# Hybrid decoder trunk: later slots for q's rstd transposes, attention steps one QKV item later, a fourth HGRN unit on unnormalised x

## The chip, the cores and the metric

The kernel runs as one program on one core of a Trainium2 chip. The metric is the device time of one execution in microseconds (us); three runs of the kernel before have a median of 2326.11 us. TensorE is called PE, VectorE DVE, ScalarE ACT, GpSimd POOL, and SyncE SP. SP issues nearly all loads.

## The reference, cut to what matters

Two layers work on a sequence of 256 tokens of width 2048 in f32. Every layer is a mixer and then a squared-ReLU MLP, each behind an RMS norm with shift, scale and gate that come from a conditioning vector. Layer 0 mixes by attention in a window of 128 tokens, layer 1 by a gated linear recurrence (HGRN2).

```python
for i in range(DEPTH):
    mod = cond @ mod_w[i] + mod_b[i]
    sh1, sc1, g1, sh2, sc2, g2 = jnp.split(mod, N_MOD, axis=-1)
    h = modulate(rms_norm(x, norm_mix[i]), sh1, sc1)
    ...
        y = swa_sink_attention(h, ...)     # layer 0
        y = hgrn2_mixer(h, ...)            # layer 1
    x = x + g1[:, None, :] * y
    h = modulate(rms_norm(x, norm_mlp[i]), sh2, sc2)
    x = x + g2[:, None, :] * squared_relu_mlp(h, mlp_w1[i], mlp_w2[i])
```

In attention, q and k get an RMS norm per head of 64 columns before the logits. In HGRN2 one projection gives q, f, v and g for 16 heads. From f come the decay and k, g gates the output, and the recurrence runs in chunks of 64 tokens.

## The kernel before

**Weights.** Every weight and every row of `mod_w` is loaded once, in pieces of 1 MB, in the order of a list that is written out by hand (`seq`, filled by `put`, L144). The pieces go through a ring of `NRAW` = 5 buffers called `raw`, and SP issues the next load when a buffer comes free. An item of kind "w" is a weight: ACT rounds each half of it to `wh`, DVE subtracts that from the original and gets `wl` (L252), and PE multiplies with both; `wh` and `wl` have 5 buffers of half an item each. An item of kind "m" is a column group of `mod_w`: one DVE instruction multiplies it with the conditioning vector and sums (L234). An item of kind "g" is another form of the same, done by PE in four small matmuls, which the profile counts as eight, with four transposes behind every fourth item (`gemv`, L259). `put` takes a function `per(i)`, which says how many such modulation items stand in the list before weight `i`.

**Order.** The program is written as one stream in Python, and a scheduler turns it into one fixed order for each engine; an instruction that is not ready by its model may be passed by later ones. Matmuls issued through `pep` are tied to the PE instruction before them, those through `pe` are not. Work that has to wait for another engine is put off with `later(n, fn)`: it is issued n slots on, and a slot passes with each call of `hook`. A unit of 32 matmuls (`mm_std`) has four slots, and so has a quarter unit of QKV (`mm_quarter`). An attention step has two.

**QKV and attention.** The projection runs in four sections, one for each quarter of the width (`s_` = 0 to 3, L863). Each has five items `e`: item 0 is k and v, items 1 to 4 are q, two tiles of four heads to an item. Only section 3 completes the sums. For the q norm, `evac_q` (L701) squares both tiles of an item; then `f1` (one slot on) sums by PE, `f2` (one slot on) turns the sums by PE transposes (`sst`), computes rstd on DVE in 13 small instructions and widens it by two copies (`widen`, L663). `f3`, once for each tile, turns the wide rstd back by four PE transposes (`spread`, tile `rbk`) and multiplies q with it (L726).

Attention is a pipeline of steps (`step`, L820). Step s forms the logits of head pair s (tile `S`), from step 1 on scales the pair before on POOL, from step 3 on transposes pair s-3 (`pt`), from step 4 on multiplies pair s-4 with v (`pv`), and from step 9 on runs the output projection for its first four tiles (`wo_step`, 12 matmuls each). Step s needs the normed q of tile s // 2. Each step also prepares up to two modulation items. With `EE` = 1 and `SE` = 3, three steps run after each of the items 2, 3 and 4 of section 3, and steps 9 to 20 run in a loop behind them. While `hold` is set, the preparation of weights does not go past a modulation item on its own.

**HGRN.** Each of 8 groups of two heads has 8 units: f, f, g, v, v, q, g, q. `start_phase` (L1032) begins the phase while the norm is still being computed: its first `count` units (`UN` = 3: f, f, g) run on x times gain and scale without rstd (`u`, three matmuls for each of 16 steps instead of two), and are multiplied with rstd afterwards. Meanwhile DVE and ACT make the 16 normed tiles `h`, with three instructions each. The first v unit is the first that needs them. Behind each q unit, `evac_hq` (L1128) computes the scaled q and k of a head into `qa`, `ka`, `qb` and `kd`, with one buffer each, and `stage1` (five slots on) has PE read them. `put` for the items `hin` (L195) spreads 32 modulation items of kind "m" over the units from item 4 on.

Of the kernel before, what the change touches and what calls it, by code (L numbers as in the profile page):

```python
# [27 lines left out]
LAG = 2  # L28
DT = 3
DV = 1  # L30
UN = 3
# [2 lines left out]
NCST = 553  # L34
LEAD = 2
GPS = 2
EE = 1
SE = 3
GD = 2


# [22 lines left out]
def trunk(ctx, tc, a, out):  # L64
# [107 lines left out]
    for c in range(3):  # L172
# [1 line left out]
        put([a["ainq"][c, i] for i in range(5)], nxt, per=lambda i: 2 * i)  # L174
    both = [e for p in zip(gga, two(0, SC2, SH2, 0, KH)) for e in p]
    put([a["ainq"][3, i] for i in range(5)] + [a["aoutk"][i] for i in range(4)], both,
        per=lambda i: (0, 0, 0, 6, 12, 18, 22, 26, 32)[i])
    order = [("o", n) for n in range(4, 12)]
    late = [("o", n) for n in range(12, 16)]
    half1 = [("u", n) for n in range(8)]  # L180
# [8 lines left out]
    for c in range(NCHUNK):  # L189
# [3 lines left out]
    put(rest, mods_of(0, G2) + two(1, SC1, SH1, 0, KB) + mods_of(1, G1),  # L193
        per=lambda i: max(0, i - 16) * 64 // 84)
    put([a["hin"][i] for i in range(64)], two(1, SC2, SH2, 0, KB),  # L195
        per=lambda i: max(0, i - 4) * 32 // 56)
    put([a["hout"][n] for n in range(16)])
    rest = []
    for c in range(NCHUNK):
# [120 lines left out]
    def later(delay, fn):  # L320
        bg.append((bgst["slot"] + delay, bgst["n"], fn))
        bgst["n"] += 1
        bg.sort(key=lambda e: (e[0], e[1]))
# [283 lines left out]
    H = feed.H  # L607
# [4 lines left out]
    with tc.tile_pool(name="attn", bufs=2) as ap:  # L612
# [88 lines left out]
        def evac_q(i, ps, part):  # L701
            dve.tensor_tensor(out=part, in0=ps, in1=part, op=ALU.add)
            sq = wt(2 * T)
            act.activation(out=sq, in_=part, func=AF.Square)
            for u in range(2):
                qts[2 * i + u] = part[:, u * T:(u + 1) * T]
                sqs.append(sq[:, u * T:(u + 1) * T])
            if i % 2 == 0:
                return
            four = sqs[:]  # L710
            sqs.clear()

            def f1():
                fin = head_rstd(four, slope2[:, 4 * i - 4:4 * i + 4])
                later(1, lambda: f2(fin))

            def f2(fin):
                r = fin()
                rxs = [widen(r, k) for k in range(2)]
                later(2, lambda: f3(rxs, 0))  # L720
                later(3, lambda: f3(rxs, 1))

            def f3(rxs, k):
                rb = spread(rxs[k])
                q = parts[i + 1 + k]
                dve.tensor_tensor(out=q, in0=q, in1=rb, op=ALU.mult)  # L726
                rq[i - 1 + k] = True
            later(1, f1)
# [364 lines left out]
    def f_tile(h):  # L1093
        if h % 2 == 0:
            cur["fl"] = htile("fl", 2, 2 * T)
            cur["kk"] = htile("kk", 2, 2 * T)
        c = slice((h % 2) * T, (h % 2 + 1) * T)
        fk[h] = (cur["fl"][:, c], cur["kk"][:, c])
        return fk[h][0]

    def g_tile(h):
        gts[h] = htile("g", 3)
        return gts[h]
# [16 lines left out]
    def evac_g(h):  # L1120
        g = gts[h]
        th = wt()
        act.activation(out=th, in_=g, func=AF.Tanh, scale=0.5)
        dve.scalar_tensor_tensor(out=g, in0=th, scalar=1.0, in1=g, op0=ALU.add, op1=ALU.mult)
        dve.tensor_scalar(out=g, in0=g, scalar1=0.5, scalar2=ogain[:, h:h + 1],
                          op0=ALU.mult, op1=ALU.mult)
# [89 lines left out]
    def evac_fg(r, h, ps):  # L1216
        if r < 2:
            total(ps, f_tile(h))
            evac_f(h)
        else:  # L1220
            total(ps, g_tile(h))
            evac_g(h)

    H, n0 = start_phase(1, 0, UN, lambda i: f_tile(i) if i < 2 else g_tile(i - 2),
                        lambda i, t: evac_f(i) if i < 2 else evac_g(i - 2))
    for i in range(n0, 64):
        G, r = divmod(i, 8)
        if r < 2:
            mm_std(H, lambda ps: evac_fg(0, 2 * G + r, ps))
        elif r in (2, 6):  # L1230
            mm_std(H, lambda ps: evac_fg(2, 2 * G + (r - 2) // 4, ps))
        elif r == 3:
            ps = mmtile()
            mm_v(H, 0, ps, True, False)
            ahead(LAG - 1, False)
        elif r == 4:
            mm_v(H, 1, ps, False, True)
            vn = hp.tile([P, 2, T], F32, tag="vn", name="vn", bufs=2)
            act.copy(out=vn.rearrange("p a b -> p (a b)"), in_=ps)
            vns[G] = vn  # L1240
            ahead(LAG - 1, False)
        else:
            mm_std(H, lambda ps: evac_hq(2 * G + (r - 5) // 2, ps))
    mod_bias(1, G1)
    prep_mods(1, SH2)
    prep_mods(1, SC2)
# [12 lines left out]
def layout(inputs):  # L1259
    import numpy as np  # L1260

    def units(w, nk):
        k, n = w.shape
        u = w.reshape(nk, KB, P, n // P, P).transpose(3, 0, 2, 1, 4)
        return np.ascontiguousarray(u.reshape((n // P) * nk, P, D))

    f = np.float32
    i = {k: np.asarray(v) for k, v in inputs.items()}
    r = {}
    r["x"] = np.ascontiguousarray(i["x"][0].T.reshape(4, 4, P, T).transpose(0, 2, 1, 3))  # L1270
    def gset(col):
        g = i["mod_w"][0][:, col * P:(col + 4) * P].reshape(4, 4, P, 2 * T)
        return g.transpose(0, 2, 1, 3).reshape(4, P, D)

    r["mod_g"] = np.stack([gset(c) for c in (0, 4, 8, 12, 32, 36, 40, 44)])
    r["mod_w"] = np.ascontiguousarray(i["mod_w"].transpose(0, 2, 1).reshape(2, 96, P, D))
    gs = np.stack([i["norm_mix"][0], i["norm_mlp"][0], i["norm_mix"][1], i["norm_mlp"][1]])
    def halves(u):
        n = u.shape[0]
        v = u.reshape(n // 2, 2, P, 2, D // 2).transpose(3, 0, 2, 1, 4)  # L1280
        return np.ascontiguousarray(v.reshape(2, n // 2, P, D))

    def vpairs(w):
        v = w.reshape(2, KB // 2, P, w.shape[1] // T, T).transpose(3, 0, 2, 1, 4)
        return np.ascontiguousarray(v.reshape(-1, 2, P, D))

    win = i["attn_w_in"][0]
    ku, qu, wv = units(win[:, D:D + T], 1), units(win[:, :D], 1), win[:, D + T:]
    def quarter(k0):
        c = slice(k0 * P, (k0 + 4) * P)  # L1290
        kv = [*ku[:, :, c], wv[k0 * P:(k0 + 4) * P].reshape(4, P, T).transpose(1, 0, 2).reshape(P, 4 * T)]
        q = qu[:, :, c].reshape(4, 4, P, 4 * P).transpose(0, 2, 1, 3).reshape(4, P, D)
        return np.concatenate([np.concatenate(kv, 1)[None], q], 0)
    r["ainq"] = np.stack([quarter(k0) for k0 in range(0, KB, 4)])
    wo = i["attn_w_out"][0]
    r["aoutk"] = np.ascontiguousarray(
        wo[:, :4 * P].reshape(4, 4, P, 4 * P).transpose(0, 2, 1, 3).reshape(4, P, D))
    r["aout"] = units(wo[:, 4 * P:], 1)
    hu = units(i["hgrn_w_in"][0], 1)
    hv = vpairs(i["hgrn_w_in"][0][:, 2 * D:3 * D])  # L1300
    hs = []
    for h in range(0, HG, 2):
        hs += [hu[16 + h], hu[17 + h], hu[48 + h], hv[h // 2, 0], hv[h // 2, 1], hu[h],
               hu[49 + h], hu[h + 1]]
    r["hin"] = np.stack(hs)
    r["hout"] = units(i["hgrn_w_out"][0], 1)
    m1 = units(i["mlp_w1"][0], 1)
    r["m1h"] = halves(m1[:16])
    r["mlp1a"] = np.ascontiguousarray(m1[16:])
    r["mlp1b"] = units(i["mlp_w1"][1], 1)  # L1310
    r["mlp2"] = np.stack([units(i["mlp_w2"][l], NCHUNK) for l in range(2)])
    kg, qg = i["attn_k_gain"][0], i["attn_q_gain"][0]
    sel = np.zeros((P, 2), f)
    sel[:HD, 0] = 1
    sel[HD:, 1] = 1
    slope = 2.0 ** (-8.0 * np.arange(1, HEADS + 1) / HEADS)
    rows = np.concatenate([i["attn_sinks"][0], (-slope).astype(f), (slope * slope / HD).astype(f),
                           np.full(4, 1.0 / HD, f)])
    cst = [i["c"].reshape(KB, P).T, np.eye(P, dtype=f), sel,
           (np.arange(P) % 32 == 0).astype(f).reshape(P, 1),  # L1320
           np.stack([np.concatenate([kg, kg]), np.concatenate([qg, qg])], 1),
           i["hgrn_o_gain"][0].T,
           np.broadcast_to(rows, (P, rows.size)),
           i["hgrn_lb_logits"].reshape(2, HG, P).transpose(2, 0, 1).reshape(P, 2 * HG),
           gs.reshape(4, KB, P).transpose(2, 0, 1).reshape(P, 4 * KB),
           i["mod_b"].reshape(2, 96, P).transpose(2, 0, 1).reshape(P, 192)]
    r["cst"] = np.concatenate(cst, 1)
    q = np.arange(P)[:, None]
    s = np.arange(P)[None, :]
    ok = s <= q  # L1330
    cur = np.where(ok, -(q - s), -1e38)
    prev = np.where(s > q, -(q + P - s), -1e38)
    r["dist"] = np.concatenate([prev, cur], 1).astype(f)
    cm = np.arange(P)[:, None] <= np.arange(P)[None, :]
    r["cmask"] = np.concatenate([cm, cm], 1).astype(np.int32)
    return r
# [20 lines left out]
```

## Time and profile before

| | us |
|---|---|
| median of 3 runs | 2326.11 (2325.68 to 2327.92) |
| the profiled execution, its own time | 2325.76 |
| span from its first to its last instruction | 2324.0 |
| PE busy | 2265.4 |
| DVE busy | 1792.2 |
| ACT busy | 1161.4 |

The profile has a page with sums and several views: busy time of each engine in stretches of time, waits by who ended them, groups of instructions by line, a timeline, and the chain of work that ended last. The busy time of PE is modelled from overlapping matmuls. PEclk is the clock that was granted to PE as a share of the full one. Idle time of an engine matters only where nothing else sets the end.

### The profile page before, as it was taken

The page shows a single profiled execution, that of the slowest core. Times are in us where ns is not written, and L with a number is a line of the kernel's source. Part 1 is how long each engine was busy: PE and PEld are TensorE (multiplying, and loading weights), DVE is VectorE, ACT ScalarE, POOL GpSimd, SP SyncE. Part 2 cuts the span into 40 slices and gives each one's busy share as a digit, 9 for nine tenths or more (in the row PEclk, how much of TensorE's full clock was granted, in tenths as well). Part 3 has the DMA queues.
Part 4 walks back from the last instruction along what each step waited for, and adds up shares of the span by engine and source line. Part 5 has one row for each costly group of instructions (what it writes and reads, how often), then busy time and mean ns, then how long its engine had stood idle before and what let it go on. Part 6 is the DMA issues. An engine that isn't in the chain of part 4 may idle for free.

```text
span 2324.0 us, 37074 instructions
## 1 busy us (share of the span) xinstructions
PE 2265.4 (97%) x14690; PEld 1988.7 (86%) x14690; DVE 1792.2 (77%) x2908; ACT 1161.4 (50%) x1962; POOL 107.8 (5%) x94
## 2 busy tenths in 40 slices
PE   5998899999999999999999999999999999999999
PEld 3885699988888888888889988999888888888888
DVE  5787798957888988988988988767766766655665
ACT  3544554644444444455666666655544444444443
POOL 0244510000000000000000000000000000000000
PEclk8998999999999999999999999999999999999999
DMA  9987799557898998975677777554666666555552
GB/s 357 399 324 276 284 351 337 203 186 269 324 335 322 331 329 329 329 288 184 219 274 268 255 269 269 186 174 171 235 237 228 242 235 233 202 185 196 181 199 91
DMA packets 84638, 598.80 MB, mean 258 GB/s; under 512 B 9456, under 2 KB 11504, under 8 KB 12272
## 3 DMA queue, kind: packets, MB, share of 16 engines
q1 hardware_dynamic: 81936, 593.81, 70.6%
q8 instruction: 115, 1.88, 0.3%
q10 hardware_dynamic: 2304, 2.10, 0.3%
q0 software_dynamic: 224, 0.52, 0.1%
q14 instruction: 59, 0.48, 0.1%
HBM read 594.04 MB, written 2.10 MB: 257 GB/s over the span
## 4 chain that ended last, share of the span: by engine, by line
PE 93%; DVE 4%; DMA 2%; ACT 1%; issue 1%; POOL 0%; DVEq 0%; ACTq 0%
PE mm L52 88%; DVE wl L252 1%; DVE raw L234 1%; PE A L52 1%; DMA raw<-in_mod_w_dram 1%; PE S L52 1%; PE on L52 0%; PE pt L52 0%; ACT wh L52 0%; PE pv L52 0%; DMA raw<-in_aoutk_dram 0%; DMA raw<-in_ainq_dram 0%; ACT h L52 0%; PE rbk L52 0%; PE cb L52 0%
## 5 line engine op out<-in xcount | busy, mean ns | idle before, releaser
L252 DVE TENSOR_TENSOR wl<-raw,wh 128x1024 fp32r<-128x1024 f32 x744 | 914.3, 1234 | 398.9 <-ACT wh L52 397.3
L52 ACT CAST wh<-raw 128x1024 fp32r<-128x1024 f32 x744 | 778.1, 1051 | 877.5 <-PE mm L52 768.0
L52 PE MATMUL mm<-h,wh 128*128 128x512 f32 (+2 forms) x3728 | 1150.7, 367 | 15.6 <-ACT wh L52 14.5
L52 PE MATMUL mm<-h,wl 128*128 128x256 f32 (+1 forms) x3232 | 906.4, 281 | 1.0 <-DVE wl L252 1.0
L52 PE MATMUL mm<-o,wh 128*128 128x512 f32 (+2 forms) x3120 | 859.0, 346 | 1.2 <-ACT o L52 0.9
L52 PEld LDWEIGHTS mm<-h,wh 128*128 128x128 f32 x3728 | 668.7, 189 | 143.2 <-ACT wh L52 15.3
L52 PE MATMUL mm<-o,wl 128*128 128x256 f32 (+1 forms) x2432 | 678.5, 280 | 0.0
L52 PEld LDWEIGHTS mm<-h,wl 128*128 128x128 f32 x3232 | 610.4, 189 | 8.2 <-issue 5.4
L52 PEld LDWEIGHTS mm<-o,wh 128*128 128x128 f32 x3120 | 538.7, 188 | 82.9 <-issue 2.2
L52 PEld LDWEIGHTS mm<-o,wl 128*128 128x128 f32 x2432 | 457.2, 188 | 0.7 <-issue 0.3
L234 DVE CUSTOM_DVE_ANT_0 raw<-raw,cond 128x2048 f32<-128x2048 f32 x160 | 368.9, 2306 | 25.5 <-DMA raw<-in_mod_w_dram 25.2
L52 ACT COPY w<-mm 128x256 f32<-128x256 f32 (+1 forms) x308 | 118.2, 386 | 24.0 <-PE mm L52 24.0
L52 PE MATMUL mm<-wh,h 128*128 128x256 f32 x576 | 106.8, 285 | 4.2 <-DVE h L553 2.7
L52 PEld LDWEIGHTS mm<-wh,h 128*128 128x128 f32 x576 | 89.8, 190 | 7.8 <-DVE h L553 3.2
L52 PE MATMUL mm<-wl,h 128*128 128x256 f32 x288 | 81.4, 283 | 0.0
L772 POOL TENSOR_SCALAR h<-h,asm 128x128 f32<-128x128 f32 x64 | 66.0, 1049 | 65.1 <-DVE qw L137 28.2
L52 ACT CAST h<-w 128x256 fp32r<-128x256 f32 x125 | 49.8, 403 | 27.5 <-DVE w L969 26.7
L52 PEld LDWEIGHTS mm<-wl,h 128*128 128x128 f32 x288 | 54.7, 190 | 0.2
L969 DVE SCALAR_TENSOR_TENSOR w<-w 128x256 f32<-128x256 f32 x125 | 52.2, 423 | 2.2
L478 DVE TENSOR_TENSOR h<-w,h 128x256 fp32r<-128x256 f32 x125 | 51.7, 419 | 0.0
L474 DVE TENSOR_TENSOR w<-mm,w 128x256 f32<-128x256 f32 x109 | 45.6, 419 | 0.4 <-ACT w L52 0.3
L990 DVE TENSOR_TENSOR acc<-mm,acc 128x256 f32<-128x256 f32 x96 | 40.6, 423 | 6.4 <-PE mm L52 3.5
(191 smaller groups left out, 1091.1 us busy)
## 6 DMA issues: line engine op xcount, KB each, us to landing
raw<-in_mod_w_dram SPq DMA_DIRECT2D x160, 1024.0 KB, 6.3
raw<-in_mlp_dram SPq DMA_DIRECT2D x128, 1024.0 KB, 4.9
raw<-in_hin_dram SPq DMA_DIRECT2D x64, 1024.0 KB, 5.0
raw<-in_mlp1b_dram SPq DMA_DIRECT2D x64, 1024.0 KB, 4.8
raw<-in_mlp1a_dram SPq DMA_DIRECT2D x48, 1024.0 KB, 6.4
raw<-in_mod_g_dram SPq DMA_DIRECT2D x32, 1024.0 KB, 6.9
raw<-in_ainq_dram SPq DMA_DIRECT2D x20, 1024.0 KB, 7.6
raw<-in_m1h_dram SPq DMA_DIRECT2D x16, 1024.0 KB, 6.7
```

The costliest lines, as they stand in the source:

```text
L52: r = fn(*args, **kw)
L234: dve.tensor_tensor_reduce(out=r, in0=r, in1=cond, scale=1.0, scalar=0.0, op0=ALU.mult, op1=ALU.add, accum_out=mods[:, e[1], e[2]:e[2] + 1])
L252: dve.tensor_tensor(out=wl, in0=part, in1=wh.bitcast(F32), op=ALU.subtract)
L474: dve.tensor_tensor(out=out_t, in0=ps[:, :T], in1=t, op=ALU.add)
L478: dve.tensor_tensor(out=opt[:, T:2 * T], in0=src_t, in1=opt[:, :T].bitcast(F32), op=ALU.subtract)
L772: pool_q.tensor_scalar(out=Ls[hh][:, cut[b]], in0=Ls[hh][:, cut[b]], scalar1=ri[:, i:i + 1], scalar2=None, op0=ALU.mult)
L969: dve.scalar_tensor_tensor(out=t, in0=t, scalar=0.0, in1=t, op0=ALU.max, op1=ALU.mult)
L990: dve.tensor_tensor(out=acc[n], in0=ps[:, :T], in1=acc[n], op=ALU.add)
```

## The change

Five edits. (1) In `evac_q`, the two `f3` of an item are issued 5 and 6 slots behind `f2` instead of 2 and 3, and for the first q item 3 and 4. (2) `EE` = 2 and `SE` = 4: the attention steps begin behind item 3 of section 3 instead of item 2, with four steps behind item 3 and four behind item 4; steps 8 to 20 follow in the loop. (3) The modulation items of that section are spread to match: none before weight 3, 8 before weight 4, 16 before the first output weight, instead of 6, 12 and 18. (4) The HGRN phase begins with four units on unnormalised x, and the order in the first group is f, f, g, g, v, v, q, q; the other groups keep theirs, and the weights are laid out to match. (5) The 32 modulation items of the HGRN phase are spread from item 12 on instead of item 4, and end at the same item 60.

```diff
-EE = 1
-SE = 3
+EE = 2
+SE = 4
...
     put([a["ainq"][3, i] for i in range(5)] + [a["aoutk"][i] for i in range(4)], both,
-        per=lambda i: (0, 0, 0, 6, 12, 18, 22, 26, 32)[i])
+        per=lambda i: (0, 0, 0, 0, 8, 16, 20, 24, 32)[i])
...
     put([a["hin"][i] for i in range(64)], two(1, SC2, SH2, 0, KB),
-        per=lambda i: max(0, i - 4) * 32 // 56)
+        per=lambda i: max(0, i - 12) * 32 // 48)
...
                 rxs = [widen(r, k) for k in range(2)]
-                later(2, lambda: f3(rxs, 0))
-                later(3, lambda: f3(rxs, 1))
+                d = 3 if i == 1 else 5
+                later(d, lambda: f3(rxs, 0))
+                later(d + 1, lambda: f3(rxs, 1))
...
-    H, n0 = start_phase(1, 0, UN, lambda i: f_tile(i) if i < 2 else g_tile(i - 2),
+    H, n0 = start_phase(1, 0, 4, lambda i: f_tile(i) if i < 2 else g_tile(i - 2),
                         lambda i, t: evac_f(i) if i < 2 else evac_g(i - 2))
+    first, other = "ffggvvqq", "ffgvvqgq"
     for i in range(n0, 64):
         G, r = divmod(i, 8)
-        if r < 2:
-            mm_std(H, lambda ps: evac_fg(0, 2 * G + r, ps))
-        elif r in (2, 6):
-            mm_std(H, lambda ps: evac_fg(2, 2 * G + (r - 2) // 4, ps))
-        elif r == 3:
+        kinds = first if G == 0 else other
+        h = 2 * G + kinds[:r].count(kinds[r])
+        if kinds[r] in "fg":
+            mm_std(H, lambda ps: evac_fg(0 if kinds[r] == "f" else 2, h, ps))
+        elif kinds[r] == "q":
+            mm_std(H, lambda ps: evac_hq(h, ps))
+        elif h == 2 * G:
...
-        hs += [hu[16 + h], hu[17 + h], hu[48 + h], hv[h // 2, 0], hv[h // 2, 1], hu[h],
-               hu[49 + h], hu[h + 1]]
+        v = [hv[h // 2, 0], hv[h // 2, 1]]
+        hs += [hu[16 + h], hu[17 + h], hu[48 + h]]
+        hs += [hu[49 + h], *v, hu[h], hu[h + 1]] if h == 0 else [*v, hu[h], hu[49 + h], hu[h + 1]]
```

More of the change, by code (lines that the diff above doesn't have):

```diff
@@ L1222, in evac_fg @@
             evac_g(h)
-    H, n0 = start_phase(1, 0, UN, lambda i: f_tile(i) if i < 2 else g_tile(i - 2),
+    H, n0 = start_phase(1, 0, 4, lambda i: f_tile(i) if i < 2 else g_tile(i - 2),
                         lambda i, t: evac_f(i) if i < 2 else evac_g(i - 2))
+    first, other = "ffggvvqq", "ffgvvqgq"
     for i in range(n0, 64):
         G, r = divmod(i, 8)
-        if r < 2:
-            mm_std(H, lambda ps: evac_fg(0, 2 * G + r, ps))
-        elif r in (2, 6):
-            mm_std(H, lambda ps: evac_fg(2, 2 * G + (r - 2) // 4, ps))
-        elif r == 3:
+        kinds = first if G == 0 else other
[5 more added lines that the diff above has]
+        elif h == 2 * G:
             ps = mmtile()
             mm_v(H, 0, ps, True, False)
-            ahead(LAG - 1, False)
-        elif r == 4:
+            ahead(LAG - 1)
+        else:
             mm_v(H, 1, ps, False, True)
@@ L1240, in trunk @@
             vns[G] = vn
-            ahead(LAG - 1, False)
-        else:
-            mm_std(H, lambda ps: evac_hq(2 * G + (r - 5) // 2, ps))
+            ahead(LAG - 1)
     mod_bias(1, G1)
```

## The prediction

> **What bounds the kernel now.** I read the page first: the share of PE, then its clock by slices.
>
> ```profile
> span 2324.0 us, 37074 instructions
> ...
> PE 2265.4 (97%) x14690; PEld 1988.7 (86%) x14690; DVE 1792.2 (77%) x2908; ACT 1161.4 (50%) x1962; POOL 107.8 (5%) x94
> ...
> PEclk8998999999999999999999999999999999999999
> ```
>
> PE is busy nearly throughout, so only places where it is not can give time. The waits of PE by cause (total us, times, longest) say where:
>
> ```profile
> PE rbk L52 <- DVE w L663: 18.4, 5, 6.5
> ...
> PE mm L52 <- DVE h L553: 2.7, 2, 1.8
> PE mm L52 <- ACT h L52: 2.6, 5, 0.9
> PE A L52 <- DVE qa L1150: 1.8, 1, 1.8
> ```
>
> The first row is q's rstd transposes (edits 1 and 2), the next two the start of HGRN (edits 4 and 5), the last one its end. Then the busy time by stretches. The columns are length, then busy us and count of PE, of its weight loads, DVE, ACT and POOL, then granted clock, DMA share and GB/s:
>
> ```profile
> 172.00:192.40 20.40, 12.67 (x88) 6.21 (x88) 17.75 (x59) 7.14 (x23) 5.36 (x5) 0.83 0.66 239
> 192.40:198.40 6.00, 6.00 (x52) 5.83 (x52) 4.76 (x12) 2.45 (x10) 5.73 (x6) 1.00 1.03 433
> 198.40:219.00 20.60, 14.68 (x94) 8.41 (x94) 15.94 (x50) 10.41 (x31) 13.20 (x11) 0.83 0.63 225
> 219.00:226.80 7.80, 7.80 (x70) 6.35 (x68) 4.06 (x9) 2.45 (x10) 2.99 (x4) 1.00 0.85 302
> 226.80:246.80 20.00, 13.51 (x93) 7.97 (x86) 16.51 (x45) 10.00 (x31) 9.11 (x7) 0.85 0.82 303
> 246.80:307.50 60.70, 59.38 (x485) 41.86 (x483) 43.76 (x114) 36.63 (x117) 29.59 (x34) 0.99 0.81 302
> ```
>
> In order these are steps 0 to 2, q item 3, steps 3 to 5, q item 4, steps 6 and 7 with the wait ahead of step 8, and steps 8 to 20. The first five are 74.8 us, in which PE is busy 12.67 + 6.00 + 14.68 + 7.80 + 13.51 = 54.7 and DVE 17.75 + 4.76 + 15.94 + 4.06 + 16.51 = 59.0. From 246.8 on PE is full. The four waits stand in the timeline, with their cause at the first:
>
> ```profile
> 171.59 0.38 PE L52 MATMUL sst<-cst,w 128*128 128x128 f32 x2
> ...
> 173.38 2.28 DVE L234 CUSTOM_DVE_ANT_0 raw<-raw,cond 128x2048 f32<-128x2048 f32 x1
> ...
> 176.91 0.76 DVE L663 COPY w<-qw 128x512 f32<-128x512 f32 x2
> ...
> 177.49 1.94 PE L52 MATMUL rbk<-cst,w 128*128 128x128 f32 x8 [5.52 <-DVE w L663]
> ```
>
> ```profile
> 190.16 1.17 PE L52 MATMUL rbk<-cst,w 128*128 128x128 f32 x8 [2.11 <-DVE w L663]
> ...
> 210.85 1.97 PE L52 MATMUL rbk<-cst,w 128*128 128x128 f32 x8 [4.08 <-DVE w L663]
> ...
> 242.08 1.94 PE L52 MATMUL rbk<-cst,w 128*128 128x128 f32 x8 [6.49 <-DVE w L663]
> ```
>
> The sums are turned at 171.59, the widened rstd is there only at 177.5, because DVE fits a modulation column of 2.28 us in between, and PE has no unpinned matmul left to run. The waits add up to 5.52 + 2.11 + 4.08 + 6.49 = 18.2 us.
>
> **The clock.** The three waits over 4 us are followed by half clock, here the first one, and the same work costs more there than later (chain of work, start and us):
>
> ```profile
> 175.90:182.70 6.80, 5.09 (x26) 2.86 (x26) 5.09 (x11) 2.01 (x4) 0.00 (x0) 0.50 0.54 172
> ```
>
> ```profile
> 180.63 2.34 PE S L52 x10
> ...
> 191.32 1.18 PE S L52 x10
> ```
>
> The rbk rows show the same: 1.94 to 1.97 us in these places and 1.17 behind the wait of 2.11, where the clock stayed. With one rbk and one S group each, half clock costs about (0.8 + 1.2) x 3 = 6 us of PE in this stage.
>
> **The change, attention (edits 1 to 3).** q item 3 moves ahead of the first step, so its 48 matmuls (6.00 us) lie between `sst` of item 1 and its `rbk`, and from then on `f3` comes 5 slots, that is 2.5 steps, behind `f2`. At 20.4 / 3 = 6.8 us a step now, or about 5 after, 2.5 steps are 12 us, against the 5.9 us from 171.59 to 177.49 with which DVE answers. I cost the four waits at 0. Their cover is the work of those steps; where it is gone, the 18.2 us come back.
>
> What is late next is DVE. Its groups from 172 to 246.8 (busy us, mean ns, idle before):
>
> ```profile
> L234 DVE CUSTOM_DVE_ANT_0 raw<-raw,cond 128x2048 f32<-128x2048 f32 x9 | 20.8, 2313 | 0.3 <-DMA raw<-in_mod_w_dram 0.3
> L752 DVE TENSOR_REDUCE asm<-S 128x1 f32<-128x128 f32 (+1 forms) x32 | 10.0, 350 | 8.1 <-PE S L52 8.1
> L252 DVE TENSOR_TENSOR wl<-raw,wh 128x1024 fp32r<-128x1024 f32 x6 | 7.3, 1220 | 0.8 <-ACT wh L52 0.8
> ...
> L702 DVE TENSOR_TENSOR o<-mm,o 128x512 f32<-128x512 f32 x5 | 3.5, 691 | 6.8 <-PE mm L52 6.8
> ```
>
> Ahead of step 8 stand 16 modulation items now instead of 18, so one column less, 2.3 us: 59.0 - 2.3 = 56.7 us is what DVE needs. PE needs 54.7 - 6 = 48.7. So DVE sets the pace, and the four steps between items 3 and 4, with four columns and no unit of PE beside them, are where it shows. How densely can DVE run? The densest long row of the trace is the first HGRN group:
>
> ```profile
> 1124.00:1174.00 50.00, 49.48 (x334) 43.96 (x335) 45.77 (x93) 31.53 (x62) 0.00 (x0) 0.97 0.60 211
> ```
>
> 45.77 / 50 = 0.92. So 56.7 / 0.92 = 61.6 us instead of 74.8: **-13.2**. The ends: without any idle time 56.7 (-18.1); with all 15.8 us of DVE's idle kept, 72.5 (-2.3). I take 0.92, since most of the idle time that ended with S or with a unit's matmuls (8.1 and 6.8 us) lies around PE's own waits. DMA doesn't bind: its share is 0.63 to 0.85 in the long rows, and it reached 1.03.
>
> The two items moved behind step 8 are a column, hidden in DVE's 60.7 - 43.76 = 17 us of idle time, and a "g" item on PE, which is full there:
>
> ```profile
> 255.22 1.06 PE L52 MATMUL mm<-raw,cst 128*32 128x512 f32 x8
> ```
>
> **+1.1.** On SP's queue the load of q item 3 goes past six modulation loads, and those of item 4 and of the first output weight past four and two. All are 1 MB in the same ring, so this changes who is early: the columns that DVE ran ahead of 172 now yield to the weight's two `wl`. POOL's scaling and its two k copies keep their places. The output weights are prepared by step 7 instead of step 8 and used from step 9 on: no cost.
>
> **HGRN's start (edits 4 and 5).** Rows: the units without norm, the first v unit, and its half clock:
>
> ```profile
> 1104.00:1116.70 12.70, 12.68 (x103) 12.41 (x102) 11.16 (x26) 6.12 (x7) 0.00 (x0) 1.00 0.67 248
> 1116.70:1124.30 7.60, 3.42 (x19) 2.34 (x17) 7.60 (x18) 6.31 (x10) 0.00 (x0) 1.00 0.71 276
> 1124.90:1128.20 3.30, 3.30 (x16) 3.11 (x15) 3.30 (x11) 2.47 (x6) 0.00 (x0) 0.50 0.02 5
> ```
>
> In the second row PE is idle 7.60 - 3.42 = 4.2 us, waiting for `h`, and the third costs up to 3.3 / 2 = 1.65. DVE's work from 1111.1 to 1141.5 on that:
>
> ```profile
> L553 DVE SCALAR_TENSOR_TENSOR h<-ht,mods,h 128x256 fp32r<-128x256 f32 x16 | 7.2, 477 | 0.1
> L548 DVE SCALAR_TENSOR_TENSOR ht<-x,gsc,rbs 128x256 f32<-128x256 f32 x16 | 7.0, 478 | 0.0
> L234 DVE CUSTOM_DVE_ANT_0 raw<-raw,cond 128x2048 f32<-128x2048 f32 x1 | 2.3, 2285 | 0.0
> ```
>
> A fourth unit covers 5.7 us (48 of the first row's 103 matmuls, its 12.68 us less 0.7 for `rb`, so 12.0 x 48 / 101), more than the 4.2 that were missing, and the column of 2.3 us goes out of the way. The unit has 48 matmuls instead of 32, +0.1 against a normal one of 5.6; its extra evacuation (about 0.9 us of DVE, two more operations and a small sum) takes less than the column gives. I take 4.2 + 1.65 - 0.1: **-5.8**, between -2 (the scans of f still delay `h`) and -7 (the shorter waits go too).
>
> **HGRN's rest.** The columns now come at 32 / 48 a unit instead of 32 / 56, 0.76 more in eight units, 1.7 us of DVE. A steady group:
>
> ```profile
> 1324.00:1374.00 50.00, 50.00 (x354) 44.76 (x353) 42.96 (x92) 32.23 (x63) 0.00 (x0) 1.00 0.75 272
> ```
>
> DVE goes from 43.0 to 44.7 of 50, below the 45.77 with which PE still got its work in the group above. The two q units side by side add a wait: the second one's `qa`, `ka`, `kd` and `qb` have one buffer, which `stage1` of the first head frees only five slots later, one slot into the next unit. Behind the waiting exponentials ACT holds casts for the weights, and PE waits for these one unit later. The nearest price is the one wait for `qa` that PE shows, 1.8 us. Ends: -1.8 (that wait goes) and +4; I take **+0.5**.
>
> **The sum.** -13.2 + 1.1 - 5.8 + 0.5 = -17.4. The profiled execution took 2325.76 us, 1.76 around the span of 2324.0: 2308.4. The median of the runs is 0.35 higher: **2308.7**.
>
> **The rivals.**
>
> *The steps keep their pace.* If DVE's idle time is not PE's fault, eight steps at 6.8 us (54.4), the two items (13.8) and a step 8 of the same pace (6.8) make 75.0 instead of 74.8, +1.1 behind: 2326.1 + 0.2 + 1.1 - 5.8 + 0.5 = 2322.1. For it: columns sit between the rstd instructions in the timeline. Against it: 14.9 us of DVE's idle time waited for PE. 0.13.
>
> *DVE runs dense.* 56.7 us: 2326.1 - 18.1 + 1.1 - 5.8 + 0.5 = 2303.8. For it: much of the rstd work now falls into q items, where DVE has 1.2 and 3.7 us free. 0.15.
>
> *DVE becomes the bound in HGRN.* If each of the six groups grows by all 1.7 us, +10.4: 2318.6. Against it: full PE at 45.77 of 50. 0.07.
>
> *Half clock through the steps; this is the slower side.* Without a unit of matmuls between, four steps in a row hold transposes, small matmuls and waits. If the clock falls in each and does not come back, PE's work in the eight steps, 54.7 - 13.8 - 6 = 34.9 us, takes 69.8; with the items (13.8) and the step 8 of 4.4 (34.9 / 8) that is 88.0 instead of 74.8: +13.2 + 1.1 - 5.8 + 0.5, 2335.1. Eight steps at full clock would be 34.9 + 13.8 + 4.4 = 53.1, and each at half clock adds 4.4; with HGRN's gain the kernel turns slower from the sixth on, and by 0.2% from the seventh. Against it: the half clock ended at 182.7, in the midst of steps without units, and the S group of 191.32 ran at full clock. 0.06. The Trainium skill, "TensorE: Matmul & The Clock Gate", Part 4, says that PE transposes do not count as PE activity for the clock gate; by that rule this rival is what comes. The trace has the recovery just named against it.
>
> *The change doesn't take.* The scheduler could place the transposes where they were, as it passes tied instructions anyhow; then only HGRN changes, 2320.8. 0.04.
>
> **How the numbers follow.** The forecast has 0.55: by itself 2304 to 2316. The range goes on to the denser DVE below and to HGRN's cost and most of the unchanged cases above: 2299 to 2321. A measurement of this kernel tells about 0.2% (4.7 us) from no change. Faster: 0.55 + 0.15 + 0.07 + 0.04 and a small part of the steady pace, 0.83. Within: the rest of that, 0.10. Slower: 0.06 and a little for a worse pace than assumed, 0.07.
>
> **What would show it.** The row of waits for `rbk` falls below 4 us, and no half clock stands between 172 and 250. Step 8 begins near 233 instead of 246.8, with DVE at 0.9 ahead of it; PE is full from there. PE's waits for `h` at 1116 vanish, and HGRN's groups stay at 50 us. I am wrong if PE's waits for rstd turn into waits for logits' buffers of equal length, or if waits for `wh` or `wl` appear in HGRN.

## The result and the profile after

The changed kernel takes 2315.18 us (median of four runs, 2313.67 to 2316.55) against 2327.02 for the kernel before beside it: 11.8 us less, a ratio of 0.995 (95% interval 0.9932 to 0.9968). The forecast was 2308.7, 17.4 us less, so the direction holds, the time lies in the range, and two thirds of the gain came. The profiled execution took 2313.67 us, with a span of 2311.9, 12.1 below that of before.

The waits of PE by cause (total us, times, longest): one more row of the kernel before, then those of the kernel after, to be held against the four rows of before:

```profile
PE mm L52 <- ACT wh L52: 14.5, 2, 14.3
```

```profile
PE mm L52 <- ACT wh L52: 17.4, 3, 14.3
...
PE rbk L52 <- DVE w L663: 3.7, 2, 3.4
PE rbk L52 <- DVE asm L755: 2.6, 1, 2.6
...
PE A L52 <- DVE qa L1151: 1.0, 2, 0.7
...
PE mm L52 <- ACT h L52: 0.4, 1, 0.4
PE mm L52 <- DVE h L553: 0.3, 1, 0.3
```

The waits ahead of q's rstd transposes (`rbk`) fell from 18.4 to 6.3 us, of which 3.7 are still for rstd, and those for `h` from 5.3 to 0.7 (from 4.2 to 0.3 at HGRN's start). But the row for `wh` grew from 14.5 to 17.4 us; nearly all of it was, and is, the wait of 14.3 at the kernel's start. The 2.9 us that are new have a place of their own, below.

The busy time by stretches in the kernel after (columns as in the prediction). The first five rows run from 172 to the start of step 8, and the sixth from there to the end of step 20:

```profile
172.00:181.00 9.00, 5.63 (x41) 4.57 (x40) 6.76 (x20) 1.52 (x3) 0.35 (x1) 0.85 0.56 204
181.00:187.20 6.20, 4.63 (x20) 1.71 (x18) 3.92 (x12) 1.63 (x3) 0.00 (x0) 0.50 0.04 15
187.20:207.20 20.00, 16.74 (x99) 7.76 (x97) 12.80 (x54) 8.57 (x30) 6.14 (x7) 0.80 0.52 184
207.20:213.10 5.90, 5.90 (x53) 5.90 (x51) 4.83 (x13) 2.59 (x14) 5.07 (x6) 1.00 1.02 428
213.10:234.20 21.10, 20.29 (x160) 10.73 (x158) 19.42 (x66) 13.61 (x46) 14.85 (x14) 1.00 0.77 291
172.00:234.20 62.20, 53.20 (x362) 30.66 (x362) 47.72 (x162) 27.92 (x94) 26.42 (x26) 0.86 0.61 229
234.20:300.40 66.20, 62.27 (x481) 41.89 (x478) 51.92 (x120) 38.31 (x134) 46.33 (x40) 0.97 0.97 361
```

From 172 to step 8 it takes 62.2 us instead of 74.8, but steps 8 to 20 take 66.2 instead of 60.7: 12.6 us gained, 5.5 given back. In the last row DVE does 51.92 us instead of 43.76, and PE idles 3.9 us instead of 1.3.

What is left of the waits for rstd is one at the first item, with the same cause as before. In the timeline a modulation column still sits in DVE's chain, and PE has only the last part of q item 3 to run behind the sums, 19 of its 48 matmuls, from 173.37 to 175.87; the others had run ahead of them:

```profile
173.24 0.38 PE L52 MATMUL sst<-cst,w 128*128 128x128 f32 x2
...
174.87 2.29 DVE L234 CUSTOM_DVE_ANT_0 raw<-raw,cond 128x2048 f32<-128x2048 f32 x1
...
175.59 0.28 PE L52 MATMUL mm<-h,wl 128*128 128x256 f32 x1
...
178.67 0.76 DVE L663 COPY w<-qw 128x512 f32<-128x512 f32 x2
...
179.24 1.09 PE L52 MATMUL rbk<-cst,w 128*128 128x128 f32 x4 [3.37 <-DVE w L663]
```

From 178.3, still within the wait, the clock is halved for 13.7 us (the second stretch above shows 0.50). A second half clock, of 3.4 us, follows the other wait, of 2.60 us, at 195.3. That one is not a wait for rstd, which was widened long before:

```profile
184.37 2.28 DVE L234 CUSTOM_DVE_ANT_0 raw<-raw,cond 128x2048 f32<-128x2048 f32 x1
...
186.69 0.33 SPq L213 DMA_DIRECT2D raw<-in_ainq_dram  x1
...
188.32 0.76 DVE L663 COPY w<-qw 128x512 f32<-128x512 f32 x2
...
191.54 1.99 ACT L52 CAST wh<-raw 128x1024 fp32r<-128x1024 f32 x2 [3.78 <-DMA raw<-in_ainq_dram]
...
192.62 1.22 DVE L252 TENSOR_TENSOR wl<-raw,wh 128x1024 fp32r<-128x1024 f32 x1 [3.53 <-ACT wh L52]
...
195.02 0.16 DVE L652 SCALAR_TENSOR_TENSOR qw<-sst,cst 128x8 f32<-128x8 f32 x1
...
195.32 1.04 PE L52 MATMUL rbk<-cst,w 128*128 128x128 f32 x4 [2.60 <-DVE asm L755]
```

The two copies of rstd were done at 189.1. But `rbk` and `sst` share two buffers in PSUM, the memory that PE writes to (tag `sp`, L646 and L668), and by these the transposes for the item's second tile needed the one that held item 3's sums. DVE read those sums only at 195.02, because `wl` of q item 4's weight stood ahead in its order, waiting for ACT's cast, and the cast for a load that SP issued at 186.69, just behind the end of a modulation column. The trace names a DVE instruction 0.1 us later as the one that ended the wait; that it was the reading of the sums is inferred from the buffers.

The place where the gain goes back, first PE, then ACT, in the timeline:

```profile
288.36 0.88 PE L52 MATMUL pt<-cst,h 128*128 128x128 f32 x6
292.11 0.74 PE L52 MATMUL mm<-o,wh 128*128 128x256 f32 x4 [2.88 <-ACT wh L52]
293.37 0.39 PE L52 MATMUL mm<-o,wl 128*128 128x256 f32 x1 [0.53 <-DVE wl L252]
...
295.43 1.55 PE L52 MATMUL pv<-PT,vnat 128*64 128x256 f32 x8
```

```profile
287.69 0.59 ACT L52 COPY w<-mm 128x512 f32<-128x512 f32 x1 [1.84 <-PE mm L52]
...
289.42 0.49 ACT L52 ACTIVATE h<-S,asm 128x256 f32<-128x256 f32 x1
...
290.88 0.23 ACT L52 CAST swt<-mods 128x8 fp32r<-128x8 f32 x1
290.99 2.02 ACT L52 CAST wh<-raw 128x1024 fp32r<-128x1024 f32 x2
```

The last output weight landed at 285.1 by the trace; its cast runs at 290.99, behind the exponentials of the last pair and `swt`, the first instruction of the MLP. PE waits 2.88 + 0.53 us, and a half clock of 3.4 us comes 2.3 us behind the first wait: the `pv` group in it takes 1.55 us, where other groups of eight take 0.80. In the kernel before, ACT was there ahead of the same weight and cast it as it landed (294.26), with the exponentials and `swt` behind it:

```profile
294.28 2.00 ACT L52 CAST wh<-raw 128x1024 fp32r<-128x1024 f32 x2 [3.06 <-DMA raw<-in_aoutk_dram]
...
302.25 0.28 ACT L52 CAST swt<-mods 128x8 fp32r<-128x8 f32 x1
```

HGRN's start and a steady group, to compare with before:

```profile
1112.00:1120.00 8.00, 8.00 (x69) 8.00 (x68) 8.00 (x19) 7.53 (x12) 0.00 (x0) 1.00 0.47 145
1120.00:1137.00 17.00, 16.68 (x117) 15.20 (x116) 16.82 (x36) 11.91 (x22) 0.00 (x0) 1.00 0.48 180
...
1312.00:1362.00 50.00, 50.00 (x354) 44.75 (x353) 44.76 (x94) 32.16 (x63) 0.00 (x0) 1.00 0.73 274
```

PE and DVE are both full or nearly so, without a half clock, and a steady group has 44.76 us of DVE, as worked out (44.7), with PE at 50 of 50.

### The profile page after: what moved, and what is told of

Same layout as the page of the kernel before. It is cut to its first block, busy times and chain, and to the rows that moved or that the text cites. A ratio compares the mean times of both kernels' runs of the same rounds, so it can differ in the third digit from the quotient of the medians.

```text
span 2311.9 us, 37115 instructions
## 1 busy us (share of the span) xinstructions
PE 2267.4 (98%) x14706; PEld 1987.3 (86%) x14706; DVE 1795.3 (78%) x2910; ACT 1161.2 (50%) x1961; POOL 114.7 (5%) x94
## 4 chain that ended last, share of the span: by engine, by line
PE 92%; DVE 5%; DMA 1%; ACT 1%; issue 1%; DVEq 0%; ACTq 0%
PE mm L52 88%; DVE wl L252 1%; DVE raw L234 1%; PE A L52 1%; DMA raw<-in_ainq_dram 1%; PE S L52 1%; PE on L52 0%; DMA raw<-in_mod_w_dram 0%; PE pv L52 0%; ACT wh L52 0%; PE pt L52 0%; ACT h L52 0%; DVE h L553 0%; DVE ht L548 0%; DVE asm L753 0%
## 5 line engine op out<-in xcount | busy, mean ns | idle before, releaser
L52 PE MATMUL mm<-h,wh 128*128 128x512 f32 (+2 forms) x3712 | 1143.3, 367 | 15.1 <-ACT wh L52 14.5
L773 POOL TENSOR_SCALAR h<-h,asm 128x128 f32<-128x128 f32 x64 | 72.4, 1147 | 52.0 <-DVE qw L139 31.9
```

What stands on the lines that cost most here:

```text
L52: r = fn(*args, **kw)
L773: pool_q.tensor_scalar(out=Ls[hh][:, cut[b]], in0=Ls[hh][:, cut[b]], scalar1=ri[:, i:i + 1], scalar2=None, op0=ALU.mult)
```

## Experiments

Four places in each trace split the kernel: the start of step 8's logits, the start of the last product with v, the last update of x in layer 0's MLP, and the length of HGRN, from there to the first update of x behind it. From HGRN's end on, every kernel takes 797.8 to 798.0 us. The time is the median of several runs for before, after, attn, hgrn and best, and a single run for the others; the places come from one profiled execution of each. Beside the single runs, the kernel before took 2326.34 us (u4, mods12, rowdve, wo28) and 2331.35 us (swt, rowswt, gearly), and 2325.78 in the median (slots, noslots), so the places say more than the single times.

| kernel | time | step 8 | last pv | MLP 0 ends | HGRN | span |
|---|---|---|---|---|---|---|
| before | 2327.02 | 246.8 | 306.6 | 1098.8 | 427.3 | 2324.0 |
| after | 2315.18 | 234.2 | 299.6 | 1093.4 | 420.6 | 2311.9 |
| attn | 2318.11 | 233.2 | 298.6 | 1092.2 | 424.4 | 2314.6 |
| hgrn | 2319.02 | 248.9 | 308.2 | 1100.4 | 420.7 | 2319.0 |
| slots | 2317.93 | 232.1 | 300.2 | 1092.6 | 425.6 | 2316.2 |
| noslots | 2326.10 | 238.5 | 312.6 | 1105.4 | 421.0 | 2324.3 |
| u4 | 2320.04 | 244.7 | 305.0 | 1097.2 | 423.1 | 2318.3 |
| mods12 | 2323.72 | 246.5 | 309.4 | 1101.6 | 422.5 | 2322.0 |
| rowdve | 2328.39 | 247.2 | 314.1 | 1108.1 | 420.7 | 2326.6 |
| wo28 | 2312.31 | 233.3 | 296.2 | 1091.8 | 420.9 | 2310.5 |
| swt | 2314.70 | 235.2 | 301.1 | 1094.6 | 420.4 | 2312.9 |
| rowswt | 2318.74 | 235.2 | 304.0 | 1098.5 | 420.5 | 2317.0 |
| gearly | 2310.08 | 228.7 | 296.2 | 1089.7 | 420.7 | 2308.3 |
| best | 2307.44 | 227.6 | 290.5 | 1086.0 | 420.7 | 2304.7 |

A part of the kernel that is not changed is not the same in each execution either: with attention as before, MLP 0 ends at 1097.2 to 1101.6 (before, hgrn, u4, mods12), and HGRN as before takes 424.4 to 427.3 us (before, attn, slots). Differences below these spreads are not read.

**attn** has edits 1 to 3, **hgrn** edits 4 and 5, each on the kernel before.

> Edits 1 to 3 alone, HGRN as before. The profiles of before and after differ by 12.6 us at the start of step 8 (246.8 against 234.2), by 7.0 us at the last product with v (306.6 against 299.6) and by 5.8 at the end of the first MLP's opening. If the two halves of the change are independent, this kernel shows the same: step 8 near 234, a wait of PE for wh of about 2.9 us near 290 with a half clock behind it, and a time 6 to 7 us below before. Rival: the wait near 290 is an accident of one execution; then it is missing here, and the time is 10 to 12 us below.

> Edits 4 and 5 alone, attention as before. By the difference of the profiles behind the attention (5.8 us at 400 us, 12.1 at the end): 6 us below before, with PE's waits for h at the start gone and no half clock there. By the forecast's terms: 5.8 - 0.5 = 5.3. Rival: what was gained in HGRN came from the other state in which attention left the loads; then it is under 3 us.

attn takes 2318.11 us against 2325.78 (ratio 0.9961, 0.9948 to 0.9974), hgrn 2319.02 (0.9974, 0.9956 to 0.9993): 7.7 and 6.8 us less. The wait near 290 comes again in attn, at 291.19 with 2.87 us, so it belongs to the order and is no accident. The wait at the first item (3.37 us) and the one at 194.4 (2.64 us) come again too. Both halves hold by themselves. Their sum of 14.5 us is above the 11.8 of the whole, within the intervals.

**slots** and **noslots** part edit 1 from edits 2 and 3:

```diff
 slots: the kernel before
-                later(2, lambda: f3(rxs, 0))
-                later(3, lambda: f3(rxs, 1))
+                d = 3 if i == 1 else 5
+                later(d, lambda: f3(rxs, 0))
+                later(d + 1, lambda: f3(rxs, 1))
 noslots: the kernel after, with these lines the other way round
```

> Edit 1 alone in the kernel before: f3 in later slots, steps still begin behind item 2. Theory: step s needs the normed q of tile s // 2 at once, and three steps per item leave no slots, so the transposes are only pushed onto the slots in which the step waits for them: PE's wait for rbk stays at 12 us or more, and step 8 begins at 240 or later. Rival: the later slots by themselves hide the chain of rstd; then the wait falls under 5 us and step 8 begins before 238.

> The whole change without edit 1: f3 again 2 and 3 slots behind f2, steps begin behind item 3. Theory: the first item's wait is covered by item 3 in any case, but those of items 2 to 4 come back, with 8 to 14 us of PE waiting for rbk, two or three half clocks, and step 8 some 5 to 10 us later than in after (240 to 245). Rival: the order of steps alone does it; then the wait for rbk stays near the 6 us of after and step 8 begins at 234 to 236.

PE's waits for `rbk`, first in slots, then in noslots:

```profile
PE rbk L52 <- DVE w L663: 7.9, 3, 5.5
```

```profile
PE rbk L52 <- DVE w L663: 10.0, 4, 5.2
PE pt L52 <- POOL h L772: 7.1, 8, 2.6
```

In slots my theory fell: the later slots alone bring step 8 to 232.1 and MLP 0 to 1092.6, as early as all three edits (1092.2). What stays is the wait at the first item, 5.5 us, and one of 2.2 at item 4, together more than the 5 us of the rival. In noslots the sum of the waits is as expected, but only the second item's comes back (5.2 us; item 3 has 1.1 and item 4 none), and the first item's, which was to be covered, stays at 3.35. Step 8 is at 238.5, earlier than expected and 4.3 us later than in after; all of that comes ahead of the first logits (192.5 against 187.2). Behind it come waits for POOL's scaled probabilities; MLP 0 ends at 1105.4, later than in any execution with attention as before. So the later slots carry the gain in attention. Starting the steps one item later adds nothing that these single runs can tell on top of them, and in noslots, without them, MLP 0 ends later than before.

**u4** and **mods12** part the two HGRN edits. u4 is hgrn with the columns from item 4 on; mods12 is the kernel before with one line changed:

```diff
-        per=lambda i: max(0, i - 4) * 32 // 56)
+        per=lambda i: max(0, i - 12) * 32 // 48)
```

> Edit 4 alone: attention as before, four units without norm and the new order of the first group, the modulation columns from item 4 on as before. Theory: the fourth unit covers PE's missing h (4.2 us of waits in the profile of before), and the column of 2.3 us that stays in the way can still show: 4 to 6 us below before. Rival: the cover comes from moving the columns; then waits for h of 2 us or more stay, and the gain is under 3.

> Edit 5 alone: attention and unit order as before, the columns from item 12 on. Theory: DVE has 2 columns less to do while it makes h (2.3 us each), so PE's waits for h fall from 4.4 us to 1 to 3, and HGRN gains 1 to 3.5 us. Rival: the columns sat in idle time of DVE; then the waits stay at 4 us and the time is as before.

PE's waits for `h` in the v units are 4.2 us before, 0.7 in u4 and 0.25 in mods12, so either edit alone covers most of them, mods12 more than expected. In their place PE waits there for `wh` and `wl`, 1.7 us in u4 and 1.1 in mods12, and not at all with both edits. HGRN takes 423.1 and 422.5 us, and 420.4 to 421.0 with both, against 424.4 to 427.3 with neither: some 5 us together, and 1 to 5 alone.

**The wait near 290.** Four runs look for its cause. rowdve moves the copies of the gemv rows from ACT to DVE, wo28 puts the last output weight four items earlier:

```diff
 rowdve
-            act.copy(out=row, in_=gv)
+            dve.tensor_copy(out=row, in_=gv)
 wo28
-        per=lambda i: (0, 0, 0, 0, 8, 16, 20, 24, 32)[i])
+        per=lambda i: (0, 0, 0, 0, 8, 16, 20, 24, 28)[i])
```

> The whole change, but the copy of a gemv result out of PSUM (the row, eight in all) is done by DVE instead of ACT. In after, that copy for the last set stands in ACT's fixed order at 287.7, waiting for PE, ahead of the last pair's exponentials, whose logits were there at 283.6, and of the cast of the last output weight, which had landed at 285.1; PE then waits 2.9 us for that cast. Theory: it is this place in ACT's order; with the copy off ACT the wait falls under 1 us, no half clock stands near 295, and the last product with v comes 3 to 5 us earlier than in after (295 to 297). Rival: the load is late; the wait stays at 2 us or more.

> The whole change with the last output weight four items earlier in the list (behind 28 instead of 32). Rival of the theory on ACT's order: if what counts is when the load is issued and cast, the cast is done before 285, the wait of 2.9 us is gone, and the last product with v comes near 295. By the theory on ACT's order it is gone as well, because a cast that is ready earlier is placed ahead of the row's copy; the two part only where the copy off ACT alone does not remove it. If neither removes it, both are wrong.

In rowdve the wait stays, at 4.27 us, so the row's copy is not the one cause; the cast now stands behind `swt`, which waits for the last column. (All eight copies are on DVE there, and the stretch ahead of the attention is 11 us longer: the first logits start at 198.5 instead of 187.2.) In wo28 the wait and the half clock are gone, and step 8 to the last pv takes 62.9 us instead of 65.4. A wait of 1.26 us for `o` (287.8) stands there instead, and MLP 0 ends 1.6 earlier than in after, which is inside the spread.

**swt** and **rowswt** take these two out of the cast's way:

```diff
 swt
-        act.copy(out=sw[:, :n, 0], in_=c)
+        dve.tensor_copy(out=sw[:, :n, 0], in_=c)
 rowswt: this, and
-            act.copy(out=row, in_=gv)
+            if col == 44:
+                dve.tensor_copy(out=row, in_=gv)
+            else:
+                act.copy(out=row, in_=gv)
```

> The whole change with one small cast for the MLP (swt, 128 x 8) moved from ACT to DVE. In rowdve the wait for the cast of the last output weight stayed, at 4.3 us, and there the cast stood in ACT's order behind swt, which waited for the last modulation column. In after swt ran at once (290.88) and the cast behind it, but both stood behind the last pair's exponentials. Theory: ACT's fixed order has two things ahead of that cast, either of which is enough: the row's copy with the exponentials behind it, and swt. Then with swt alone removed the wait stays at 2 to 3 us. Rival: swt is the one cause; then it is gone.

> The whole change with swt on DVE and the copy of the last gemv row alone on DVE too (the other seven stay on ACT). Theory of the two: PE's wait for wh near 290 falls under 1 us, the half clock behind it is gone, and the last product with v comes 3 to 5 us earlier than in after, counted from the start of step 8 (61 to 63 us instead of 65.4 behind it). Rival: the load of the last output weight is too late in itself (issued at 278.3, landed at 285.1); then the wait stays at 2 us or more.

swt keeps the wait (2.79 us), as expected. But rowswt does too, with 4.91, so the theory of two causes fell as well. ACT's timeline there:

```profile
290.83 0.87 ACT L52 COPY PT<-pt 128x384 f32<-128x384 f32 x2
294.48 0.19 ACT L52 CAST h<-swt 128x2 fp32r<-128x2 f32 x1 [2.79 <-DVE swt L579]
294.58 1.99 ACT L52 CAST wh<-raw 128x1024 fp32r<-128x1024 f32 x2
```

The next instruction of the MLP's start, `h` from `swt`, has taken the place of `swt`. The weight had landed at 286.4 by the trace; its cast comes at 294.58. What after, rowdve and rowswt have in common is that the weight stands behind all 32 modulation items of the list, and that ACT's order has the first instructions of the MLP, which need the last column, ahead of its cast. wo28 takes the weight out from there, and the wait goes. The place in the list is not enough by itself: before, slots and noslots have the same one, their casts come 8 us and more ahead of `swt`, and PE does not wait for them. What it takes is ACT's order; why the scheduler turned it round in the kernel after, these runs do not show. That the load is late in itself, the rival, has against it the 5.9 and 8.2 us from landing to cast in after and rowswt.

**gearly** is meant to test whether DVE's sum of work sets step 8: the 16 g and 16 m items come in another order, 10 g and 6 m ahead of step 8.

```diff
-    both = [e for p in zip(gga, two(0, SC2, SH2, 0, KH)) for e in p]
+    gm = (iter(gga), iter(two(0, SC2, SH2, 0, KH)))
+    both = [next(gm[int(k)]) for k in "00100101" * 2 + "10110101" * 2]
```

> The whole change with the order of modulation items altered: of the 16 ahead of step 8, 10 are done by PE and 6 by DVE instead of 8 and 8, and the reverse behind it. Theory: ahead of step 8 DVE sets the pace while PE is idle 9.8 us, and behind it PE is full while DVE is idle, so two columns of 2.3 us moved behind and two items of 1.06 us moved ahead gain 2 to 4 us at step 8 (230 to 232 instead of 234.2) and 2 us behind it: 2 to 6 us in all. Rival: step 8 is set by the chain from rstd to the logits and not by DVE's sum of work; then step 8 stays within 1.5 us of 234, and only the 2 us behind it, or nothing, are gained.

Two rows of the waits of gearly, the one for `wh`, with the wait behind step 8 in it, and the one for `rbk`; then its stretch from 172 to step 8:

```profile
PE mm L52 <- ACT wh L52: 21.1, 4, 14.3
...
PE rbk L52 <- DVE w L664: 0.7, 2, 0.4
```

```profile
172.00:228.70 56.70, 52.22 (x396) 31.08 (x395) 47.88 (x163) 29.51 (x102) 26.70 (x25) 1.00 0.74 272
```

Step 8 starts at 228.7, 5.5 us earlier than in after and more than expected, but not by the theory: DVE does as much in this stretch as in after (47.88 us against 47.72; one column less, one `wl` and one sum at L703 more). What went are the waits ahead of `rbk`, from 6.3 to 0.7 us, with no column left between the first item's sums (171.9) and its `rbk` (175.3), and the half clocks: none stands between 172 and 250. So the rival's mechanism, the chain from rstd, is what this run speaks for, though step 8 moved. The 2 us behind step 8 did not come; the wait for the last output weight grew to 4.86 us and ate them.

**best** is gearly and wo28 together.

> The whole change with both alterations: 10 and 6 instead of 8 and 8 items ahead of step 8, and the last output weight behind 28 items instead of 32. In gearly step 8 came at 228.7 but PE then waited 4.9 us for the cast of the last output weight, which landed at 281.5 and stood in ACT's order behind the first instructions of the MLP (swt), which need the last column; in rowswt it stood behind the next of them (h from swt) in the same way. Theory: the cast's place behind the last column costs these 4.9 us and the half clock behind, and with the weight ahead of the last four items the kernel comes to 2305 to 2309, faster than after (2315.2) and than wo28 and gearly alone (2312.3, 2310.1). Rival: the waits only move on, as in wo28, where 2.5 us came off ahead of the last product with v and under half of it was left at the MLP; then it is 2309 to 2312.

It takes 2307.44 us, as expected (2306.43 to 2308.33, five runs), a ratio of 0.9916 to before (0.9903 to 0.993), outside the interval of after. Step 8 starts at 227.6, the last pv at 290.5, and no half clock is left between the one near the kernel's start and the one at its end. At the end of MLP 0 the two alterations give 3.7 and 1.6 us alone, each inside the spread of 4.4, and 7.4 together.

## Why the prediction was right, and where it was not

**Bound.** PE was the bound and its waits were the time to be had. That held: the gain is where the rows of waits stood.

**The first five stretches, -13.2: measured -12.6, by another way.** The step "DVE sets the pace", 56.7 us of work at 0.92, gave 61.6; measured are 62.2. But DVE did only 47.7 us in them, at 0.77, so its sum of work did not set the pace. Six columns ran between 172 and step 8, not eight, and three `wl` instead of six; two of the other three had moved ahead of 172. Behind step 8 DVE does 8.2 us more than before (51.92 against 43.76), where the forecast moved 2.3. And two of the four waits ahead of `rbk`, costed at 0, were left: they cost 6.0 us and were accompanied by 17 us of half clock. Two errors cancelled, which was luck. gearly, with DVE's sum as in after, takes 5.5 us more off this stretch: what counts there is where DVE's long instructions stand in the chain, and not how much DVE has to do.

**What covers the waits.** The forecast gave the first wait to q item 3 and the others to the later slots. The first of these steps failed: "its 48 matmuls (6.00 us) lie between `sst` of item 1 and its `rbk`", but 19 of them did, 2.5 us. The chain from `sst` to `rbk` took 6.0 us (173.24 to 179.24), as it took 5.9 before, and 3.37 of that were left as a wait. The later slots held: in slots the waits for rstd of items 2 and 3 are gone without the new order of steps, and 2.2 us of item 4's are left. The wait of 2.60 in after came from the load of a weight, through DVE's order; the sentence on SP's queue, "this changes who is early", had the cause and gave it no price.

**Behind step 8, +1.1: measured +5.5.** This is the term that was missed. "The output weights are prepared by step 7 instead of step 8 and used from step 9 on: no cost" looked at the first of them and not at the last. Its place in the list, behind all 32 items, is kept by the change, but its cast came behind the MLP's first instructions in ACT's order: 56.8 us after the start of step 8 instead of 47.5, with the landing at 50.9 instead of 47.5. Of the 4.4 us that were missed, 2.88 + 0.53 are the wait for its cast, and the half clock behind, 3.4 us long, costs up to 1.7.

**HGRN's start, -5.8, and its rest, +0.5: together -5.3.** Measured are 6.8 in the run by itself, with an interval from 1.6 to 10, and about 5 in HGRN's stretch against the mean of the three executions without the edits (425.8 - 420.6). At HGRN's start the waits for `h` went from 4.2 to 0.3 us and the half clock went. The wait for `qa` that I priced for the two q units side by side is not there: `stage1` of the first group's second head has no wait, and PE's waits for `qa` are 1.0 us in all, in later groups. Waits for `wh` or `wl`, the sign of being wrong there, do not appear in HGRN.

**The rivals.** The slower one, half clock through the steps, did not come. The row from 213.1 to 234.2 has four steps of logits, transposes and small matmuls at a granted clock of 1.00. The Trainium skill, "TensorE: Matmul & The Clock Gate", Part 4, has transposes not count as activity in the way that matmuls do. In this row they do no harm: they are 7.1 of PE's 20.29 busy us, among other small matmuls. The trace does not tell whether they run in the transpose mode that the page speaks of, and no run here has a stretch of transposes alone. Ahead of that row the clock did fall, both times beside a wait, so in this trace the half clock goes with the waits and not with the transposes. HGRN did not become bound by DVE (50.00 of 50 at 44.76).

## What to carry to other kernels

Where several engines work through fixed orders, a wait that is covered moves on to the next fixed order: after covering one, look at the last item of each list that the change re-spaced, and not at the first, and at what stands ahead of it on the engine that prepares it. When a short chain on one engine gates another, putting its consumer later helps at once, and moving long instructions of the same engine out of the chain helped on top of it here. An engine's sum of work says little about the pace while it is not full: at 0.77 busy, it was the place of its long instructions that counted. And look at where the work that is to cover a wait really stands in the order: of 48 matmuls, 19 stood behind the sums.

## What the runs showed of the hardware

Short waits went with a halved clock too. Before, in the attention, a wait of 2.11 us left the clock as it was, and the halved ones came with waits of 4.08 us and more; but at HGRN's start a half clock (1124.8) followed four waits of 0.53 to 1.79 us, 4.2 us in all within 8. After, the waits of 3.37 and 2.88 us each had a half clock, the first from 178.3, before the wait had ended, the second 2.3 us behind it; and the one of 2.60 at 195.3 too, which began only shortly after another half clock had ended. In slots, waits of 2.23 and 2.35 us (236.1 and 297.5) had none. The half clocks in these traces, but for those cut off by the kernel's end, last 3.4, 6.8, 10.2, 13.7, 17.1 or 23.9 us, nearly multiples of 3.4.
